# Three edits to a two-layer streaming encoder step: the order of the first tile's work, three copies out of PSUM in place of three sums, and a V load moved behind a K load

## The chip, the cores and the metric

The program runs on one core of one Trainium2 chip. The metric is the device time of one execution in microseconds: 1293.45 us is the median of three runs of the kernel before (1292.77 to 1294.03).

## What is computed

One inference step of a trunk with two layers, for two groups of rows that share all weights: a prompt of 512 rows and a sample group of 8 x 16 = 128 rows, together 640 rows of 1024 numbers, held as five tiles of 128 rows. Layer 0 mixes rows by chunked gating, layer 1 by attention with a forget bias over 16 heads, where the sample rows also read 256 cached rows of K and V for each of 8 sequences. Cut to what matters here:

```python
for i in range(DEPTH):                       # DEPTH = 2
    hp = rms_norm(xp, norm_pre[i])           # the same for the sample rows
    if i % N_MIXERS == 0:
        op, _ = gmlp_branch(hp, ...)
    else:
        qp, kp, vp, zp, lfp = fox_project(hp, fox_w_in[j], fox_b_f[j])
        op = (fox_attend_prompt(qp, kp, vp, lfp) * jax.nn.silu(zp)) @ fox_w_out[j]
        # sample rows: fox_attend_sample with cache_fox_k, cache_fox_v, cache_fox_logf
    xp = xp + rms_norm(op, norm_post[i])
    xp = xp + jax.nn.sigmoid(xp @ ple_w_gate[i]) * (p_prompt[i] @ ple_w_proj[i])
```

## The kernel before

**Split products.** Every fp32 factor of a large product is held as a high part (a ScalarE copy into a reduced fp32 format) and a low part (VectorE: source minus high part). `split` (line 286) makes both, and `mm3` (line 270) sums three matmuls of the parts in PSUM; lines 272 to 274 are most of TensorE's work. So each weight costs ScalarE one pass (line 289, or 292 with a scale) and VectorE one (line 290 or 293) before TensorE can use it.

**Seven products.** The large projections of both layers use a scheme that makes a 2 x 2 block product from seven block products in place of eight (`seven_products`, line 558). On the weights' side its sums are made by GpSimd (line 211). On the side of the activations the normalised rows h, transposed and stored split as `h_hi` and `h_lo`, are cut into four quarters: `quarter(i, j)` holds channels of half i (`c` in the transposes, 512 of 1024) and rows of half j (320 of 640). `right_operands` (line 428) first restores the four quarters as hi + lo (line 434, four VectorE adds of 128 x 1280), then forms four differences (line 436) and splits three of them into the tile `tb` (`tbf` in layer 1); the fourth is split later over `quarter(0, 1)`. `sums_of_h` (line 1175) calls it at the start of layer 1.

**The start.** The first rows come in as ten half tiles on the DMA queues. For tile t VectorE and ScalarE square one half each (lines 402 and 401), GpSimd takes a power of the sum (line 302), VectorE scales the two halves (line 409), TensorE transposes four blocks for each half (line 316, PSUM banks 5 to 7 in turn), and the transposed half is split into `A`, which holds `h_hi` and `h_lo`. Between these stand the splits of the first weights (`prefetch`). Three matmuls on zeros stand ahead of all (line 388).

**Between the layers.** `tail` (line 635) ends layer 0. In its last loop each tile of the new x is normalised and transposed by `norm_to_hT` (line 320), which fills `h_hi` and `h_lo` for layer 1.

**Layer 1.** After the first v, k and q, seven passes of one loop (lines 1189 to 1193) each project z of head pair p and v, k, q of pair p + 1 (4 x 12.35 in the code's own time units), with the attention of pair p as pieces between the matmuls at given due times (`interleave`, line 357). The cached K comes as four loads for two heads and two groups of four sequences, in pieces of 128 bytes, into one buffer (`kraw`); `turn_k` (line 1052) transposes it on VectorE (line 1056) into `kt`, and only then may the next K load write. The cached V comes by `load_v` (line 1046), two DMAs of 512 KB for one group, into one buffer `vv` that the matmuls of line 1107 read. The projections' weights come on GpSimd's DMA queue (source fox_w_in), everything named here on SyncE's. The forget bias of a head goes through memory (`c_sc`, `cs_sc`) and comes back to the `sff` tile or to the constants' tile `CST`; line 996 uses it, then lines 1006 and 1009 (score minus bias, minimum), 1012 (exponential), 1016 and 1017 (normalise) and 1023 (transposes on TensorE).

**What sets the order.** The program is written in one order and a scheduler with a timeline model chooses the order on each engine; `queued(e)` (line 127) ties the instructions inside it behind the one that was noted last for engine e. An engine runs its own instructions in that order and waits at each for what it needs. SyncE's DMA issues are one such row: an issue that waits holds back all later ones.

Of the kernel before, what the change touches and what calls it, by code (L numbers as in the profile page):

```python
# [57 lines left out]
def hybrid_trunk(tc, x_prompt, x_sample, ck, cv, clf, p_prompt, p_sample, norm_pre, norm_post,  # L58
# [6 lines left out]
    N_WARM = 3  # L65
# [220 lines left out]
    def split(hi, lo, src, times=None):  # L286

        if times is None:
            nc.scalar.activation(out=hi, in_=src, func=AF.Copy)  # L289
            nc.vector.tensor_tensor(out=lo, in0=src, in1=f(hi), op=ALU.subtract)  # L290
        else:
            nc.scalar.activation(out=hi, in_=src, func=AF.Copy, scale=times)
            nc.vector.scalar_tensor_tensor(out=lo, in0=src, scalar=times, in1=f(hi), op0=ALU.mult, op1=ALU.subtract)  # L293

# [16 lines left out]
    def transposed_split(src, hi_of, lo_of, banks):  # L311

        for c in range(2):
            b = bank(banks)
            for j in range(4):
                nc.tensor.transpose(out=b[:, j * P:(j + 1) * P], in_=src[:, (4 * c + j) * P:(4 * c + j + 1) * P], identity=ident)  # L316
            bv = b.rearrange("p (k n) -> p k n", k=4)
            split(hi_of(c), lo_of(c), bv)

    def norm_to_hT(x, junk, xn, gpre, t, banks):  # L320
        ss = small()
        nc.scalar.activation(out=junk, in_=x, func=AF.Square, accum_out=ss)
        rs = rstd_of(ss, RMS_EPS)
        nc.vector.scalar_tensor_tensor(out=xn, in0=x, scalar=rs, in1=gpre, op0=ALU.mult, op1=ALU.mult)

        transposed_split(xn, lambda c: h_hi[:, 4 * c:4 * c + 4, t * P:(t + 1) * P],
                         lambda c: h_lo[:, 4 * c:4 * c + 4, t * P:(t + 1) * P], banks)
# [68 lines left out]
    for h in range(2):  # L396
        nc.tensor.matmul(gb[h], ones, grow[:, h * 512:(h + 1) * 512], start=True, stop=True)
    for t in range(NT):
        x, xn = r2(t * D, D), r2(5120 + (t % 2) * D, D)
        ss = [small(), small()]  # L400
        nc.scalar.activation(out=xn[:, :512], in_=x[:, :512], func=AF.Square, accum_out=ss[0])
        nc.vector.scalar_tensor_tensor(out=xn[:, 512:], in0=x[:, 512:], scalar=1.0, in1=x[:, 512:], op0=ALU.mult, op1=ALU.mult,
                                       accum_out=ss[1])
# [3 lines left out]
        for h in range(2):  # L407
            hs = slice(h * 512, (h + 1) * 512)
            nc.vector.scalar_tensor_tensor(out=xn[:, hs], in0=x[:, hs], scalar=rs, in1=gb[h], op0=ALU.mult, op1=ALU.mult)
        transposed_split(xn, lambda c: h_hi[:, 4 * c:4 * c + 4, t * P:(t + 1) * P],  # L410
                         lambda c: h_lo[:, 4 * c:4 * c + 4, t * P:(t + 1) * P], (5, 6, 7))
        prefetch(t + 1)
# [15 lines left out]
    def right_operands(at):  # L428

        b11, b12, b21, b22, t_a = (r1(o, 1280).rearrange("p (k n) -> p k n", k=4) for o in at)  # L430
        t_b = b11
        for q, (i, j) in zip((b11, b12, b21, b22), ((0, 0), (0, 1), (1, 0), (1, 1))):
            hi, lo = quarter(i, j)
            nc.vector.tensor_tensor(out=q, in0=f(hi), in1=f(lo), op=ALU.add)
        for o, a, b, dst in ((t_a, b12, b11, 0), (t_b, b22, t_a, 1), (b21, b21, t_b, 2), (b12, b22, b12, None)):
# [3 lines left out]
        return b12  # L439
# [713 lines left out]
    def attention_pieces(p, step, s1):  # L1153
# [8 lines left out]
        if p < 7:  # L1162
            pieces += [(s1 + 18, lambda: store_y(2 * p)), (s0 + kb + 0.2, lambda: load_k(p + 1, 0, 0)), (s1 + 13.5, lambda: load_v(p + 1, 0))]
# [4 lines left out]
    def next_keys(p, t, t_new):  # L1168

        return [(t, lambda: turn_k(p, 0, 0)), (t + 0.1, lambda: load_k(p, 0, 1)), (t + 12, lambda: turn_k(p, 0, 1)),  # L1170
                (t + 12.1, lambda: load_k(p, 1, 0)), (t_new, lambda: new_k(p, 0))]
# [3 lines left out]
    def sums_of_h():  # L1175
        sums.append(right_operands((o_P, o_v + 1280, o_q, o_qp, o_z)))
# [61 lines left out]
```

## Time and profile before

| what | value |
|---|---|
| median of three runs | 1293.45 us (1292.77 to 1294.03) |
| the profiled execution | 1294.02 us, of it the span of the trace 1292.2 us |
| TensorE (PE) busy | 1272.2 us, 98% |
| VectorE (DVE) busy | 967.8 us, 75% |
| ScalarE (ACT) busy | 588.0 us, 46% |
| GpSimd (POOL) busy | 362.8 us, 28% |
| moved by DMA | 171.53 MB, of 275265 packets 188761 are under 512 B |

Times in the trace count from the start of the span. A row of the timeline gives start, duration, engine, line, operation, what it writes and reads, and in brackets how long the engine sat idle before it and what ended that. PEld is TensorE's load of the stationary factor. A "q" behind an engine's name is its sequencer, which issues DMAs. The view of windows gives the busy time of each engine in a stretch, with the number of its instructions, then the granted TensorE clock, the busy share of the 16 DMA engines and GB/s. The view of waits lists for each pair of waiting line and releaser the sum, the number of times and the longest.

### The profile page before, as it was taken

The numbers are of one execution on the slowest core, as the hardware profiler recorded it, in microseconds if no ns is written. First come the engines' busy times: TensorE is split into PE (matmuls) and PEld (weight loads), VectorE is DVE, ScalarE is ACT, GpSimd is POOL, SyncE is SP. The second block draws the span as 40 slices with busy tenths as digits, with TensorE's granted clock in tenths as the row PEclk, the third lists the DMA queues.
The fourth block names the chain that finished last, engine by engine and source line by source line (L and its number), as shares of the span: only waits on it lengthen the run. The fifth ranks groups of instructions, "written<-read, shape, count | busy, mean of one in ns | idle before, by whom it ended". The sixth has DMA issues, their size and how long they took to land. (4 is left out here: it accounts for less than half of the span.)

```text
span 1292.2 us, 21109 instructions
## 1 busy us (share of the span) xinstructions
PE 1272.2 (98%) x7873; PEld 1140.7 (88%) x7873; DVE 967.8 (75%) x1808; ACT 588.0 (46%) x1062; POOL 362.8 (28%) x328
## 2 busy tenths in 40 slices
PE   8999999999999999998999999999989999999998
PEld 6888999999988888887899999999979999788887
DVE  7844999999944375798988898989878988644643
ACT  5433555444535353454544454545444444545331
POOL 1012445453000010345444535454525430000100
PEclk9999999999999999999999999999999999999999
DMA  6432343332324212648797758787868758732111
GB/s 231 131 99 81 109 125 118 91 97 89 118 98 149 80 55 92 153 87 166 160 172 159 187 150 184 161 167 140 175 103 192 176 112 248 266 126 82 66 61 55
DMA packets 275265, 171.53 MB, mean 133 GB/s; under 512 B 188761, under 2 KB 238473, under 8 KB 275162
## 3 DMA queue, kind: packets, MB, share of 16 engines
q1 hardware_dynamic: 261170, 127.80, 36.2%
q0 software_dynamic: 10080, 36.89, 14.1%
q10 hardware_dynamic: 3912, 5.50, 1.4%
q8 instruction: 62, 1.02, 0.3%
q14 instruction: 41, 0.34, 0.1%
HBM read 148.55 MB, written 21.59 MB: 132 GB/s over the span
## 5 line engine op out<-in xcount | busy, mean ns | idle before, releaser
L272 PE MATMUL pb<-A,W 128*128 128x320 f32 (+1 forms) x752 | 240.9, 320 | 0.4 <-ACT A L289 0.4
L273 PE MATMUL pb<-A,W 128*128 128x320 f32 (+1 forms) x752 | 234.4, 312 | 1.0 <-DVE A L290 1.0
L274 PE MATMUL pb<-A,W 128*128 128x320 f32 (+1 forms) x752 | 234.0, 311 | 0.6 <-DVE W L293 0.5
L290 DVE TENSOR_TENSOR W<-RAW,W 128x1024 fp32r<-128x1024 f32 (+1 forms) x126 | 151.6, 1204 | 74.8 <-ACT W L289 72.2
L272 PE MATMUL pb<-W,A 128*128 128x512 f32 x520 | 204.4, 394 | 2.6 <-ACT A L289 2.6
L273 PE MATMUL pb<-W,A 128*128 128x512 f32 x520 | 203.1, 391 | 0.0
L274 PE MATMUL pb<-W,A 128*128 128x512 f32 x520 | 202.6, 393 | 0.0
L289 ACT ACTIVATE W<-RAW 128x1024 fp32r<-128x1024 f32 (+1 forms) x126 | 120.1, 953 | 95.7 <-PE pb L274 47.6
L273 PEld LDWEIGHTS pb<-A,W 128*128 128x128 f32 x752 | 142.1, 189 | 1.6 <-DVE A L290 1.3
L272 PEld LDWEIGHTS pb<-A,W 128*128 128x128 f32 x752 | 142.0, 189 | 1.5 <-ACT A L289 0.7
L274 PEld LDWEIGHTS pb<-A,W 128*128 128x128 f32 x752 | 141.6, 188 | 1.1 <-DVE W L293 1.1
L302 POOL TENSOR_TENSOR SML<-SML 128x1 f32<-128x1 f32 x25 | 17.7, 710 | 374.2 <-DVE SML L300 369.5
L272 PEld LDWEIGHTS pb<-W,A 128*128 128x128 f32 x520 | 98.0, 188 | 23.0 <-ACT A L289 3.4
L272 PE MATMUL pb<-tbf,W 128*128 128x320 f32 x360 | 118.1, 328 | 0.0
L274 PEld LDWEIGHTS pb<-W,A 128*128 128x128 f32 x520 | 97.9, 188 | 20.1 <-DVE SML L300 0.2
L273 PEld LDWEIGHTS pb<-W,A 128*128 128x128 f32 x520 | 97.9, 188 | 19.6
L274 PE MATMUL pb<-tbf,W 128*128 128x320 f32 x360 | 111.6, 310 | 0.0
L273 PE MATMUL pb<-tbf,W 128*128 128x320 f32 x360 | 111.4, 309 | 0.0
L211 POOL TENSOR_TENSOR sff<-RAW 128x512 f32<-128x512 f32 x46 | 60.5, 1317 | 180.4 <-DVE W L290 113.7
L564 DVE TENSOR_TENSOR R<-R,pb 128x320 f32<-128x320 f32 x184 | 86.3, 477 | 14.7 <-PE pb L274 13.4
L290 DVE TENSOR_TENSOR A<-R,A 128x640 fp32r<-128x640 f32 (+1 forms) x42 | 35.2, 873 | 58.6 <-ACT A L289 58.2
L272 PEld LDWEIGHTS pb<-tbf,W 128*128 128x128 f32 x360 | 67.7, 188 | 9.0 <-issue 5.4
(271 smaller groups left out, 2828.9 us busy)
## 6 DMA issues: line engine op xcount, KB each, us to landing
RAW<-in_fox_w_in POOLq DMA_DIRECT2D x46, 512.0 KB, 7.1
RAW<-in_gmlp_w_in SPq DMA_DIRECT2D x40, 512.0 KB
R<-in_cache_fox_k SPq DMA_DIRECT2D x128, 128.0 KB
R<-in_cache_fox_v SPq DMA_DIRECT2D x32, 512.0 KB
RAW<-in_gmlp_w_out SPq DMA_DIRECT2D x16, 512.0 KB
RAW<-in_ple_w_gate SPq DMA_DIRECT2D x16, 512.0 KB
RAW<-in_fox_w_out SPq DMA_DIRECT2D x16, 512.0 KB
R<-in_fox_w_in POOLq DMA_DIRECT2D x14, 512.0 KB, 8.2
```

The lines of the kernel that those rows point to most:

```text
L211: nc.gpsimd.tensor_tensor(out=o, in0=a, in1=b, op=op)
L272: nc.tensor.matmul(out, lh, rh, start=start, stop=False)
L273: nc.tensor.matmul(out, lh, rl, start=False, stop=False)
L274: nc.tensor.matmul(out, ll, rh, start=False, stop=stop)
L289: nc.scalar.activation(out=hi, in_=src, func=AF.Copy)
L290: nc.vector.tensor_tensor(out=lo, in0=src, in1=f(hi), op=ALU.subtract)
L302: behind["pool"] = nc.gpsimd.tensor_tensor(out=q, in0=t, in1=mhalf, op=ALU.pow)
L564: behind["dve"] = nc.vector.tensor_tensor(out=into(i, j), in0=a, in1=b, op=ALU.add)
```

## The change

Three edits.

1. **The first tile.** Four matmuls on zeros, into a bank that is not in use yet, stand on TensorE behind the first four transposes of tile 0. On ScalarE and VectorE the squares of tile 1 are tied behind the high part of tile 0's first half and behind both scalings of tile 0; the second weight unit's split is tied behind those scalings too.
2. **h of layer 1.** `norm_to_hT` copies the transposed half from PSUM once more with ScalarE, as plain fp32, into three of the four quarters that `right_operands` wants (all but channels of half 1, rows of half 0). `right_operands` in layer 1 then adds hi + lo for one quarter in place of four. These quarters lie in other places of the buffer `R1`, and the fourth difference goes to another place. Layer 0 still makes all four adds.
3. **V behind the second K load.** `load_v(p + 1, 0)` leaves its own due time (39.5) and is tied on SyncE's queue behind `load_k(p + 1, 1, 0)`, which is due at 46.1.

```diff
--- before.py
+++ after.py
@@ -62,7 +62,7 @@
     NRAW, NW = 3, 5
     N_SMALL, N_KEPT = 192, 172
     N_R1 = 17760
-    N_WARM = 3
+    N_WARM, N_FILL = 3, 4
 
     sbuf = tc.alloc_tile_pool(name="sbuf", bufs=1)
     psum = tc.alloc_tile_pool(name="psum", bufs=1, space=PSUM)
@@ -286,11 +286,12 @@
     def split(hi, lo, src, times=None):
 
         if times is None:
-            nc.scalar.activation(out=hi, in_=src, func=AF.Copy)
+            first = nc.scalar.activation(out=hi, in_=src, func=AF.Copy)
             nc.vector.tensor_tensor(out=lo, in0=src, in1=f(hi), op=ALU.subtract)
         else:
-            nc.scalar.activation(out=hi, in_=src, func=AF.Copy, scale=times)
+            first = nc.scalar.activation(out=hi, in_=src, func=AF.Copy, scale=times)
             nc.vector.scalar_tensor_tensor(out=lo, in0=src, scalar=times, in1=f(hi), op0=ALU.mult, op1=ALU.subtract)
+        return first
 
     def rstd_of(ss, eps, mean=False, keep=False):
         t = small()
@@ -308,14 +309,19 @@
     xin_p, xin_s = x_prompt[0], x_sample.rearrange("b q d -> (b q) d")
     yo_p, yo_s = y_p[0], y_s.rearrange("b q d -> (b q) d")
 
-    def transposed_split(src, hi_of, lo_of, banks):
+    def transposed_split(src, hi_of, lo_of, banks, after=None):
 
         for c in range(2):
             b = bank(banks)
             for j in range(4):
-                nc.tensor.transpose(out=b[:, j * P:(j + 1) * P], in_=src[:, (4 * c + j) * P:(4 * c + j + 1) * P], identity=ident)
+                behind["pe"] = nc.tensor.transpose(out=b[:, j * P:(j + 1) * P], in_=src[:, (4 * c + j) * P:(4 * c + j + 1) * P], identity=ident)
             bv = b.rearrange("p (k n) -> p k n", k=4)
-            split(hi_of(c), lo_of(c), bv)
+            hi = split(hi_of(c), lo_of(c), bv)
+            if after is not None:
+                after(c, hi, bv)
+
+    KEPT = {(0, 0): 12416, (0, 1): 5120, (1, 1): 6400}
+    HT = TOK // 2
 
     def norm_to_hT(x, junk, xn, gpre, t, banks):
         ss = small()
@@ -323,8 +329,15 @@
         rs = rstd_of(ss, RMS_EPS)
         nc.vector.scalar_tensor_tensor(out=xn, in0=x, scalar=rs, in1=gpre, op0=ALU.mult, op1=ALU.mult)
 
+        def keep(c, hi, bv):
+            for j in range(2):
+                a, b = max(t * P, j * HT), min((t + 1) * P, (j + 1) * HT)
+                if a < b and (c, j) in KEPT:
+                    q = r1(KEPT[c, j], 1280).rearrange("p (k n) -> p k n", k=4)
+                    nc.scalar.activation(out=q[:, :, a - j * HT:b - j * HT], in_=bv[:, :, a - t * P:b - t * P], func=AF.Copy)
+
         transposed_split(xn, lambda c: h_hi[:, 4 * c:4 * c + 4, t * P:(t + 1) * P],
-                         lambda c: h_lo[:, 4 * c:4 * c + 4, t * P:(t + 1) * P], banks)
+                         lambda c: h_lo[:, 4 * c:4 * c + 4, t * P:(t + 1) * P], banks, keep)
 
     h_hi, h_lo = (A[:, z:z + 5120].rearrange("p (k n) -> p k n", k=8) for z in (0, 5120))
 
@@ -395,21 +408,31 @@
     gb = PB[3], PB[4]
     for h in range(2):
         nc.tensor.matmul(gb[h], ones, grow[:, h * 512:(h + 1) * 512], start=True, stop=True)
+
+    def first_tile(c, hi, bv):
+        if c == 0:
+            behind["act"] = hi
+            for i in range(N_FILL):
+                with queued("pe"):
+                    behind["pe"] = nc.tensor.matmul(PB[2][:, :256], warm[:, :P], warm[:, 256:], start=True, stop=True)
+
     for t in range(NT):
         x, xn = r2(t * D, D), r2(5120 + (t % 2) * D, D)
         ss = [small(), small()]
-        nc.scalar.activation(out=xn[:, :512], in_=x[:, :512], func=AF.Square, accum_out=ss[0])
-        nc.vector.scalar_tensor_tensor(out=xn[:, 512:], in0=x[:, 512:], scalar=1.0, in1=x[:, 512:], op0=ALU.mult, op1=ALU.mult,
-                                       accum_out=ss[1])
+        with queued(*["act", "dve"] * (t == 1)):
+            nc.scalar.activation(out=xn[:, :512], in_=x[:, :512], func=AF.Square, accum_out=ss[0])
+            nc.vector.scalar_tensor_tensor(out=xn[:, 512:], in0=x[:, 512:], scalar=1.0, in1=x[:, 512:], op0=ALU.mult, op1=ALU.mult,
+                                           accum_out=ss[1])
         sq = small()
         nc.vector.tensor_tensor(out=sq, in0=ss[0], in1=ss[1], op=ALU.add)
         rs = rstd_of(sq, RMS_EPS)
         for h in range(2):
             hs = slice(h * 512, (h + 1) * 512)
-            nc.vector.scalar_tensor_tensor(out=xn[:, hs], in0=x[:, hs], scalar=rs, in1=gb[h], op0=ALU.mult, op1=ALU.mult)
+            behind["dve"] = nc.vector.scalar_tensor_tensor(out=xn[:, hs], in0=x[:, hs], scalar=rs, in1=gb[h], op0=ALU.mult, op1=ALU.mult)
         transposed_split(xn, lambda c: h_hi[:, 4 * c:4 * c + 4, t * P:(t + 1) * P],
-                         lambda c: h_lo[:, 4 * c:4 * c + 4, t * P:(t + 1) * P], (5, 6, 7))
-        prefetch(t + 1)
+                         lambda c: h_lo[:, 4 * c:4 * c + 4, t * P:(t + 1) * P], (5, 6, 7), first_tile if t == 0 else None)
+        with queued(*["dve"] * (t == 0)):
+            prefetch(t + 1)
 
 
     o_X, o_ln, o_sum, o_th = 14208, 15232, 16256, 17216
@@ -425,18 +448,20 @@
     def right_sum(i):
         return tuple(TB[:, z:z + 4 * HT].rearrange("p (k n) -> p k n", k=4) for z in (i * 2560, i * 2560 + 1280))
 
-    def right_operands(at):
+    def right_operands(at, ready=()):
 
         b11, b12, b21, b22, t_a = (r1(o, 1280).rearrange("p (k n) -> p k n", k=4) for o in at)
         t_b = b11
+        last = t_a if ready else b12
         for q, (i, j) in zip((b11, b12, b21, b22), ((0, 0), (0, 1), (1, 0), (1, 1))):
-            hi, lo = quarter(i, j)
-            nc.vector.tensor_tensor(out=q, in0=f(hi), in1=f(lo), op=ALU.add)
-        for o, a, b, dst in ((t_a, b12, b11, 0), (t_b, b22, t_a, 1), (b21, b21, t_b, 2), (b12, b22, b12, None)):
+            if (i, j) not in ready:
+                hi, lo = quarter(i, j)
+                nc.vector.tensor_tensor(out=q, in0=f(hi), in1=f(lo), op=ALU.add)
+        for o, a, b, dst in ((t_a, b12, b11, 0), (t_b, b22, t_a, 1), (b21, b21, t_b, 2), (last, b22, b12, None)):
             nc.vector.tensor_tensor(out=o, in0=a, in1=b, op=ALU.subtract)
             if dst is not None:
                 split(*right_sum(dst), o)
-        return b12
+        return last
 
 
     def v_at(p, t):
@@ -1160,20 +1185,25 @@
         for hh in range(2):
             pieces += prompt_times(2 * p + hh, t0 + 4 * step * hh, step)
         if p < 7:
-            pieces += [(s1 + 18, lambda: store_y(2 * p)), (s0 + kb + 0.2, lambda: load_k(p + 1, 0, 0)), (s1 + 13.5, lambda: load_v(p + 1, 0))]
+            pieces += [(s1 + 18, lambda: store_y(2 * p)), (s0 + kb + 0.2, lambda: load_k(p + 1, 0, 0))]
         if p == 6:
             pieces += [(48, lambda: load_w0(14)), (48, lambda: load_w0(15))]
         return pieces
 
     def next_keys(p, t, t_new):
 
+        def load_second():
+            load_k(p, 1, 0)
+            with queued("sp"):
+                load_v(p, 0)
+
         return [(t, lambda: turn_k(p, 0, 0)), (t + 0.1, lambda: load_k(p, 0, 1)), (t + 12, lambda: turn_k(p, 0, 1)),
-                (t + 12.1, lambda: load_k(p, 1, 0)), (t_new, lambda: new_k(p, 0))]
+                (t + 12.1, load_second), (t_new, lambda: new_k(p, 0))]
 
     sums = []
 
     def sums_of_h():
-        sums.append(right_operands((o_P, o_v + 1280, o_q, o_qp, o_z)))
+        sums.append(right_operands((KEPT[0, 0], KEPT[0, 1], o_qp, KEPT[1, 1], o_P), KEPT))
 
     def first_k():
         with queued("sp"):
```

How this moves instructions, at three places. The rows give line, operation, what it writes and reads, the shape, and how many alike stand in a row; lines of the changed kernel are numbered anew (409 became 431, 402 became 424, 434 became 459, 436 became 461, 900 became 925, 300 became 301).

First, VectorE in the first microseconds, from the first scaling of tile 0 on (`r2a_t` holds rows and their scaled copies, `W` the split weights, `A` the split h, `pb_73` and `pb_74` the gains in PSUM, `pb_75` and `pb_76` transposed halves). Before:

```order
L409 SCALAR_TENSOR_TENSOR r2a_t<-r2a_t,SML,pb_73 128x512
L290 TENSOR_TENSOR W<-RAW,W 128x1024
L402 SCALAR_TENSOR_TENSOR r2a_t,SML<-r2a_t 128x512
L409 SCALAR_TENSOR_TENSOR r2a_t<-r2a_t,SML,pb_74 128x512
L405 TENSOR_TENSOR SML<-SML 128x1
L290 TENSOR_TENSOR A<-pb_75,A 128x4x128
L300 TENSOR_SCALAR SML<-SML 128x1
L402 SCALAR_TENSOR_TENSOR r2a_t,SML<-r2a_t 128x512
L409 SCALAR_TENSOR_TENSOR r2a_t<-r2a_t,SML,pb_73 128x512
L409 SCALAR_TENSOR_TENSOR r2a_t<-r2a_t,SML,pb_74 128x512
```

and with the change:

```order
L431 SCALAR_TENSOR_TENSOR r2a_t<-r2a_t,SML,pb_73 128x512
L431 SCALAR_TENSOR_TENSOR r2a_t<-r2a_t,SML,pb_74 128x512
L290 TENSOR_TENSOR W<-RAW,W 128x1024
L424 SCALAR_TENSOR_TENSOR r2a_t,SML<-r2a_t 128x512
L290 TENSOR_TENSOR A<-pb_75,A 128x4x128
L427 TENSOR_TENSOR SML<-SML 128x1
L424 SCALAR_TENSOR_TENSOR r2a_t,SML<-r2a_t 128x512
L301 TENSOR_SCALAR SML<-SML 128x1
L290 TENSOR_TENSOR W<-RAW,W 128x1024
L290 TENSOR_TENSOR A<-pb_76,A 128x4x128
L427 TENSOR_TENSOR SML<-SML 128x1
L431 SCALAR_TENSOR_TENSOR r2a_t<-r2a_t,SML,pb_73 128x512
```

The second scaling of tile 0 comes ahead of the weights' low part, the low part of tile 0's first half moves one place up, and the scalings of tile 1 now stand behind the second weights' low part and behind the low part of tile 0's second half.

Second, VectorE where layer 0 ends and layer 1 begins, from the last but one tile's low part on (`R_69` is the buffer with the quarters and differences, `A` the split h, `tbf` the split differences). Before:

```order
L434 TENSOR_TENSOR R_69<-A 128x1280
L290 TENSOR_TENSOR A<-pb_77,A 128x4x128
L290 TENSOR_TENSOR A<-pb_75,A 128x4x128
L900 TENSOR_TENSOR R_69<-R_69,pb_70 128x256
L434 TENSOR_TENSOR R_69<-A 128x1280
L900 TENSOR_TENSOR R_69<-R_69,pb_73 128x256
L434 TENSOR_TENSOR R_69<-A 128x1280
L436 TENSOR_TENSOR R_69<-R_69 128x1280 x3
L290 TENSOR_TENSOR tbf<-R_69,tbf 128x1280
```

and with the change:

```order
L290 TENSOR_TENSOR A<-pb_77,A 128x4x128
L290 TENSOR_TENSOR A<-pb_75,A 128x4x128
L925 TENSOR_TENSOR R_69<-R_69,pb_70 128x256
L461 TENSOR_TENSOR R_69<-R_69 128x1280
L925 TENSOR_TENSOR R_69<-R_69,pb_73 128x256
L461 TENSOR_TENSOR R_69<-R_69 128x1280
L290 TENSOR_TENSOR tbf<-R_69,tbf 128x1280
L461 TENSOR_TENSOR R_69<-R_69 128x1280
L290 TENSOR_TENSOR tbf<-R_69,tbf 128x1280
```

No add of line 434 is left in this stretch (the one that stays is made before the last tile's halves), and the differences start right behind the last tile's low part.

Third, SyncE's row in one pass of the layer 1 loop, from the last store of new K rows (`out`) on; the first four of the K loads are the first head of group 1 for the next pair, the next four its second head, and the second two V loads group 1. Before:

```order
L124 DMA out<-R_69 32x16x32
L124 DMA out<-R_69 32x4x32
L124 DMA R_69<-in_cache_fox_v 128x4x256 x2
L124 DMA R_69<-in_cache_fox_k 32x32x32 x8
L124 DMA R_69<-in_cache_fox_v 128x4x256 x2
```

and with the change:

```order
L124 DMA out<-R_69 32x16x32
L124 DMA out<-R_69 32x4x32
L124 DMA R_69<-in_cache_fox_k 32x32x32 x4
L124 DMA R_69<-in_cache_fox_v 128x4x256 x2
L124 DMA R_69<-in_cache_fox_k 32x32x32 x4
L124 DMA R_69<-in_cache_fox_v 128x4x256 x2
```

The first four K loads pass the two V loads; all else in this row stays.

## The prediction

> **What bounds the kernel now.** I read the page first, then TensorE's waits, the windows around each wait, and the timelines of the engines it waits for.
>
> ```profile
> PE 1272.2 (98%) x7873; PEld 1140.7 (88%) x7873; DVE 967.8 (75%) x1808; ACT 588.0 (46%) x1062; POOL 362.8 (28%) x328
> ```
>
> TensorE is busy for 98% of the span, so the edits can only win back what it loses: 1292.2 less 1272.2, 20 us, and what a wait costs behind itself. The waits say where this is.
>
> ```profile
> PE pb L272 <- DVE SML L1009: 5.6, 2, 3.8
> PE pb L272 <- ACT A L289: 3.1, 3, 2.4
> PE pb L1023 <- DVE R L1017: 1.3, 3, 0.9
> PE pb L273 <- DVE A L290: 1.0, 1, 1.0
> ```
>
> The largest sits in an attention score (L1009) and is really two waits. The second row is mostly the start. The windows place the rest.
>
> ```profile
> 10.00:20.00 10.00, 9.04 (x37) 6.95 (x38) 9.80 (x21) 5.66 (x10) 1.10 (x2) 0.83 0.89 333
> ...
> 520.00:560.00 40.00, 40.00 (x238) 34.15 (x237) 34.16 (x41) 19.09 (x34) 11.99 (x12) 1.00 0.58 149
> 560.00:580.00 20.00, 17.98 (x109) 16.55 (x108) 20.00 (x29) 12.22 (x18) 9.33 (x8) 1.00 0.43 76
> 580.00:600.00 20.00, 19.38 (x133) 16.65 (x132) 19.75 (x33) 8.22 (x12) 11.29 (x11) 1.00 0.91 158
> 600.00:620.00 20.00, 17.31 (x126) 16.02 (x124) 16.43 (x48) 8.83 (x19) 10.12 (x13) 1.00 0.80 161
> ...
> 950.00:960.00 10.00, 6.42 (x36) 5.25 (x37) 10.00 (x22) 2.65 (x7) 6.46 (x5) 0.83 0.42 64
> ```
>
> Three places: the first 20 us; the start of layer 1, where VectorE is full (20.00 of 20) and TensorE misses 2.02 + 0.62 + 2.69 = 5.3 us from 560 to 620; and one spot near 950, where TensorE misses 3.58 us and the granted clock falls to 0.83 on average. Each edit aims at one of them.
>
> **The V load behind the second K load.** The spot near 950, on VectorE and then on TensorE:
>
> ```profile
> 949.54 1.43 DVE L1056 STREAM_TRANSPOSE R<-R 128x256 f32<-128x256 f32 x4 [6.92 <-DMA R<-in_cache_fox_k]
> ...
> 953.42 0.47 PE L272 MATMUL pb<-W 128*128 128x384 f32 x1 [3.82 <-DVE SML L1009]
> ```
>
> VectorE waits 6.92 us for a K load, though all else in its row is ready, and TensorE then waits for a score behind that transpose. SyncE's row, here and three passes earlier:
>
> ```profile
> 656.63 0.95 SPq L124 DMA_DIRECT2D R<-in_cache_fox_v  x2
> 657.67 17.02 SPq L124 DMA_DIRECT2D R<-in_cache_fox_k  x8
> ...
> 749.90 0.94 SPq L124 DMA_DIRECT2D R<-in_cache_fox_v  x2
> ...
> 818.07 0.94 SPq L124 DMA_DIRECT2D R<-in_cache_fox_v  x2
> ...
> 886.24 1.01 SPq L124 DMA_DIRECT2D R<-in_cache_fox_v  x2
> ...
> 915.45 15.36 SPq L124 DMA_DIRECT2D out<-R  x16
> 930.90 0.96 SPq L124 DMA_DIRECT2D R<-in_cache_fox_v  x2
> 931.96 21.21 SPq L124 DMA_DIRECT2D R<-in_cache_fox_k  x8
> ...
> 960.24 2.63 SPq L124 DMA_DIRECT2D R<-in_cache_fox_v  x2
> ...
> 1028.81 0.94 SPq L124 DMA_DIRECT2D R<-in_cache_fox_v  x2
> ```
>
> The V loads at 749.90, 818.07, 886.24, 960.24 and 1028.81 are the same point of five passes. The passes last 68.17, 68.17, 74.00 and 68.57: the stall costs 5.83 + 0.40 = 6.2 us, more than the 3.8 us of the wait, because the half clock after it and the work left over cost too.
>
> Why is K late in this pass alone? The K loads of the next pair are issued from 931.96 on, behind 1 MB of V at 930.90. The DMA view of 938 to 946 (while K is awaited) and of 661 to 664 (the end of a K load that came in time):
>
> ```profile
> q0 software_dynamic: 229, 0.86, 76.7%
> q1 hardware_dynamic: 1156, 0.15, 11.7%
> ```
>
> ```profile
> q1 hardware_dynamic: 3591, 0.46, 97.0%
> q0 software_dynamic: 80, 0.33, 28.4%
> ```
>
> q1 is SyncE's queue, q0 GpSimd's, with the weights. Alone, K's small packets get 97% of the engines (3591 in 3 us); beside the weights 11.7% (1156 in 8 us). At 657 V and K were through before the weights came; at 931 V took the free time, and K fell among the weights. With the change K goes first: it takes the few microseconds that V had, V meets the weights. K's issue, at 931.96 + a few, then ends before the weights and well before 942.6 (949.54 less 6.92), when VectorE wants it. I take the whole of the stall, **6.2 us**; the bounds are 0 (K late all the same) and 6.2. What is late next? V: it is needed by the matmuls of line 1107, which the V reload at 960.24 follows directly. That leaves V about 25 us from 934, where alone it needs about 4. Moved with V are its two issues, 0.96 us on SyncE; K gains them. SyncE's wait for `turn_k` now also stands ahead of V, but in this pass the 16 stores until 930.81 hold both back anyway.
>
> [...] The rows give 1156 / 229, 5 small packets of q1 for each of q0. [...]
>
> **Three of h's four sums from PSUM.** Removed on VectorE in the full stretch are three adds of line 434:
>
> ```profile
> L434 DVE TENSOR_TENSOR R<-A 128x1280 f32<-128x1280 f32 x3 | 7.1, 2355 | 1.2 <-PE pb L316 1.2
> ...
> 573.17 2.29 DVE L290 TENSOR_TENSOR A<-R,A 128x1280 fp32r<-128x1280 f32 x1
> ...
> 596.76 0.67 DVE L846 COPY R<-pb 16x512 f32<-16x512 f32 x1
> ...
> 605.38 0.29 DVE L996 TENSOR_TENSOR R<-sff,CST 128x128 f32<-128x128 f32 x1 [3.56 <-DMA sff<-c_sc]
> ...
> 575.51 0.41 PE L273 MATMUL pb<-A,W 128*128 128x320 f32 x1 [0.99 <-DVE A L290]
> ...
> 607.02 0.44 PE L272 MATMUL pb<-W 128*128 128x384 f32 x1 [1.79 <-DVE SML L1009]
> ```
>
> They hold 7.1 us between 545 and 555, all of them ahead of the differences, and VectorE has no gap from there to 601. So everything behind comes up to 7 us sooner. The changed row also pulls the forget chain (lines 830 to 848, some 4 us here, estimated from their pieces between 577.95 and 593.28) ahead of the split of `quarter(0, 1)`, the A row at 573.17: that split then ends near 575.5 - 7.1 + 4 = 572.4, over 2 us ahead of the matmul at 575.51, whose 0.99 us goes, as do the two small waits just ahead of it. The copy of the forget sums (596.76), whose trip through memory ends VectorE's wait of 3.56 us at 605.38, comes well over 10 us sooner; so the 1.79 us at 607.02 go too. Sum of TensorE's waits at stake: about 2.0 (560 to 580), 1.8, and 0.9 of the L1023 row, 4.7; I take **4.3 us**, since new waits of a few tenths for the weights' splits are likely where VectorE stays full. Bounds: 0 (something else is just behind) and the 5.3 us of the windows.
>
> Added on ScalarE are nine copies, six of 128 x 512 and three of half that size. The nearest row is a high part from PSUM, 0.58 us below: 6 x 0.58 + 3 x about 0.35 (estimate) = 4.5 us over the last gate stage and the first v. From 520 to 560 ScalarE is busy for 19.09 of 40, so they fit. Each holds its PSUM bank 0.6 us longer, out of three in turn; TensorE was never idle there (40.00 of 40). If that cover fails, the last tile's transposes wait 0.6 us each, at most twice. I cost it at nothing.
>
> **The first tile.**
>
> ```profile
> 8.73 1.23 DVE L290 TENSOR_TENSOR W<-RAW,W 128x1024 fp32r<-128x1024 f32 x1 [1.96 <-ACT W L289]
> ...
> 9.22 0.58 ACT L289 ACTIVATE A<-pb 128x512 fp32r<-128x512 f32 x1
> ...
> 9.84 0.50 PE L272 MATMUL pb<-W,A 128*128 128x512 f32 x1 [2.36 <-ACT A L289]
> ...
> 11.21 0.68 DVE L290 TENSOR_TENSOR A<-pb,A 128x512 fp32r<-128x512 f32 x1
> ...
> 11.59 1.06 ACT L289 ACTIVATE W<-RAW 128x1024 fp32r<-128x1024 f32 x1 [1.18 <-DMA RAW<-in_gmlp_w_in]
> ...
> 12.77 1.41 DVE L409 SCALAR_TENSOR_TENSOR r2a_t<-r2a_t,SML,pb 128x512 f32<-128x512 f32 x2
> ```
>
> The high part of tile 0 no longer stands behind a square, so the first product starts about 0.6 us sooner; its low part (11.21) moves up by about 0.7, the scaling that stood before it. Against that, tile 1's scalings (12.77) now stand behind the second weights' low part, which cannot start before 11.59 + 1.06 = 12.65 and takes 1.23, and behind tile 0's second low part, 0.68: 14.5, later by 1.8 us. Meanwhile TensorE has the products of tile 0, but they wait for the same low part. VectorE, 9.80 of 10 busy, makes as much in the same time; the order alone wins little. The four matmuls on zeros run while TensorE would have waited for ScalarE (2.36 us at 9.84) and cost nothing. I take **0.2 us** gain; bounds 1.8 us loss and 1.7 us gain (0.7, and 1.0 if the clock, 0.83 from 10 to 20, stays up).
>
> **The sum.** 1294.02 (span 1292.2, 1.8 around it) - 6.2 - 4.3 - 0.2 = 1283.3 for an execution like the profiled one, which lies 0.57 above the median; against the median 1293.45: 1282.7 us.
>
> **The rivals.**
> - *K is late all the same* (the weights come sooner too, or another pass takes over the stall): for it speaks that weights are in flight more than half of the time; against, that K now goes 4 us sooner in all seven passes. 1282.7 + 6.2 = 1288.9.
> [...]
> - *Layer 1's start has a second bound just behind* (weights' arrival: the DMA share is 0.91 from 580 to 600): 1282.7 + 4.3 = 1287.0.
> - *Both fail*: 1293.2.
> - *V takes K's place, slower*: V behind K meets the weights in each pass and shares at 11.7%, where 4 us of V become over 30. It decides if weights stay in flight for more than about 21 of V's 25 us. The 0.86 MB in 8 us would bring a pass's 8 units of 512 KB in under 40 of 68 us, in lumps, which speaks against. If so, at an estimated 2.5 us for each of seven passes in line 1107: 1293.45 - 4.5 - 6.2 + 17.5 = 1300.
>
> **How the numbers follow.** Both large gains: 0.55, own range 1279 to 1286. K late all the same 0.12, turns by the page 0.03, second bound in layer 1 0.13, both fail 0.07, V late 0.10. About 0.2% (2.6 us) is what a measurement of this kernel can tell from no change. Faster by more than that: 0.55 + 0.12 + 0.03 + 0.13 = 0.83; same 0.07; slower 0.10. The range leaves out V late at the top and about a tenth at the bottom (all upper bounds together: 1293.45 - 6.2 - 5.3 - 1.7 = 1280.2, and as much again as the half clock adds to a wait): 1278 to 1293.2.
>
> **What would show it.** Right: no wait of L1056 for in_cache_fox_k over 1 us, seven even passes near 68.2 us; TensorE busy over 19 of 20 us in both windows from 560 to 580 and 600 to 620; first 20 us within 1 us of before. Wrong: line 1107's matmuls waiting for in_cache_fox_v, or TensorE waiting in 560 to 620 for a split of weights with VectorE idle.

## The result and the profile after

The changed kernel takes 1288.71 us (median of six runs, 1287.66 to 1289.38) against 1293.93 us for the kernel before in the same rounds: a ratio of 0.996, interval 0.9947 to 0.9973, 5.2 us. The forecast was 10.8 us, 1282.7 us.

First the page and TensorE's waits of the changed kernel (us in total, times, longest).

```profile
PE 1271.9 (99%) x7881; PEld 1140.2 (89%) x7881; DVE 962.9 (75%) x1805; ACT 592.3 (46%) x1071; POOL 356.6 (28%) x328
```

```profile
PE pb L272 <- DVE R L600: 2.5, 1, 2.5
PE pb L272 <- DVE SML L1034: 2.0, 1, 2.0
PE pb L1048 <- DVE R L1042: 1.7, 1, 1.7
PE pb L401 <- DVE r2a_t L393: 1.5, 1, 1.5
```

The 5.6 us behind a score have shrunk to one wait of 2.0 (L1034 was L1009, L600 was L575). A wait for L600, a sum of block products, is new. The windows say where:

```profile
10.00:20.00 10.00, 9.24 (x42) 5.86 (x40) 9.23 (x20) 6.53 (x13) 2.10 (x2) 1.00 0.92 341
...
560.00:580.00 20.00, 20.00 (x121) 17.75 (x120) 17.79 (x32) 10.23 (x15) 10.14 (x9) 1.00 0.46 78
580.00:600.00 20.00, 17.46 (x127) 16.27 (x126) 11.96 (x25) 6.73 (x11) 11.88 (x14) 1.00 0.89 181
600.00:620.00 20.00, 15.95 (x108) 13.55 (x108) 18.71 (x45) 9.62 (x22) 9.81 (x9) 1.00 0.73 122
...
950.00:960.00 10.00, 10.00 (x71) 8.36 (x70) 8.21 (x20) 4.93 (x11) 7.26 (x6) 1.00 0.50 71
```

Near 950 nothing is lost any more. At the start of layer 1 TensorE gained 2 us from 560 to 580, and lost 1.9 and 1.4 more in the next two windows. VectorE has more free time than before there (11.96 of 20, was 19.75), and still TensorE waits for it.

The ledger below is worked out from the traces of all the kernels run: the start of a matmul, less the start of the same one (by its count among those of its line and operands) in the trace of before, in us, at five times of before; minus is sooner. "Round" is the median less the median of before in the same rounds.

```
                                   at 35   500   700  1000  1285 | round
changed kernel (1 + 2 + 3)          0.97  1.38  1.08 -5.15 -5.57 | -5.2
e1  V alone (3)                    -0.16  0.00 -0.33 -6.56 -7.16 | -6.9
e2  h alone (2)                    -0.82 -0.81  3.55  3.41  4.61 | +5.3
e3  first tile alone (1)            0.79  1.19  0.32  0.18  0.92 | +2.6
e4  changed, sums by SyncE          1.04  1.47  2.47 -3.77 -4.52 | -3.6
e5  2 + 3                           0.09  0.24 -1.06 -7.29 -7.81 | -7.6
e6  1 + 3                           0.78  1.08  1.21 -5.02 -5.20 | -5.1
e7  3, zeros                        0.61  0.98  1.28 -4.96 -5.30 | -6.0
e8  changed, sums by ScalarE        1.89  2.33  1.41 -4.83 -4.39 | -5.7
e9  2 + 3, no way through memory   -0.37 -0.28 -4.55 -10.78 -10.78 | -10.8
e10 3, no way through memory       -0.81 -0.66 -3.09 -9.32 -9.53 | -9.2
e11 1 + 3, no zeros                 1.67  1.96  2.10 -4.13 -4.84 | -5.1
e12 2 + 3, sums by ScalarE         -0.63 -0.62 -0.43 -6.66 -7.12 | -7.1
```

In the changed kernel the first 35 us cost 1.0 us and the rest of layer 0 another 0.4, the start of layer 1 (500 to 700) gained 0.3, and the stretch with the late K load (700 to 1000) gained 6.2.

SyncE's row of the changed kernel has the same point of the passes as the five V loads of the prediction:

```profile
750.99 0.93 SPq L124 DMA_DIRECT2D R<-in_cache_fox_v  x2
...
819.15 0.94 SPq L124 DMA_DIRECT2D R<-in_cache_fox_v  x2
...
887.32 1.71 SPq L124 DMA_DIRECT2D R<-in_cache_fox_v  x2
...
932.30 2.23 SPq L124 DMA_DIRECT2D R<-in_cache_fox_k  x4
934.63 1.20 SPq L124 DMA_DIRECT2D R<-in_cache_fox_v  x2
...
955.49 3.15 SPq L124 DMA_DIRECT2D R<-in_cache_fox_v  x2
...
1023.65 0.94 SPq L124 DMA_DIRECT2D R<-in_cache_fox_v  x2
```

All four passes last 68.16 or 68.17 us; the one of 74.00 is gone.

And the start of layer 1: GpSimd's row (which issues the weights' loads and the sums' way through memory), VectorE's, TensorE's, and the DMA view's times from issue to landing in 578 to 612.

```profile
579.22 1.51 POOL L122 DMA_DIRECT2D RAW<-in_fox_w_in  x2
581.75 0.54 POOL L122 DMA_DIRECT2D c_sc<-R  x1
588.92 0.56 POOL L122 DMA_DIRECT2D sff<-c_sc  x1 [4.73 <-DMA c_sc<-R]
```

```profile
579.19 0.64 DVE L871 COPY R<-pb 16x512 f32<-16x512 f32 x1
...
594.87 0.29 DVE L1021 TENSOR_TENSOR R<-sff,CST 128x128 f32<-128x128 f32 x1 [7.74 <-DMA sff<-c_sc]
595.08 1.22 DVE L290 TENSOR_TENSOR W<-R,W 128x1024 fp32r<-128x1024 f32 x1
596.21 0.69 DVE L290 TENSOR_TENSOR W<-RAW,W 128x512 fp32r<-128x512 f32 x1
596.81 0.48 DVE L600 TENSOR_TENSOR R<-R,pb 128x320 f32<-128x320 f32 x1
...
597.35 0.41 PE L272 MATMUL pb<-A,W 128*128 128x320 f32 x1 [2.54 <-DVE R L600]
```

```profile
sff<-c_sc POOLq DMA_DIRECT2D x1, 256.0 KB, 5.9
...
c_sc<-R POOLq DMA_DIRECT2D x1, 32.0 KB, 6.9
```

Before, the same two took less:

```profile
sff<-c_sc POOLq DMA_DIRECT2D x1, 256.0 KB, 4.5
...
c_sc<-R POOLq DMA_DIRECT2D x1, 32.0 KB, 2.8
```

The forget sums are copied at 579.19 in place of 596.76, 17.6 us sooner, but VectorE has them back only 10.5 us sooner (594.87 for 605.38). Their write is now issued 2.5 us behind two weights' loads on the same queue. Of the 7.1 us between, the write takes 4.1 (6.9 for 2.8) and the read 1.4 (5.9 for 4.5); the other 1.6 pass between the copy and the issue of the write, ahead of which GpSimd's row has two loads. VectorE's row stands at line 1021 for 7.74 us, and behind that stand two splits of weights and the sum for which TensorE waits.

### The profile page after: what moved, and what is told of

Same layout as the page of the kernel before. It is cut to its first block, busy times and chain, and to the rows that moved or that the text cites. A ratio compares the mean times of both kernels' runs of the same rounds, so it can differ in the third digit from the quotient of the medians.

```text
span 1287.1 us, 21134 instructions
## 1 busy us (share of the span) xinstructions
PE 1271.9 (99%) x7881; PEld 1140.2 (89%) x7881; DVE 962.9 (75%) x1805; ACT 592.3 (46%) x1071; POOL 356.6 (28%) x328
## 4 chain that ended last, share of the span: by engine, by line
PE 94%; DVE 3%; DMA 2%; issue 0%; ACT 0%; SPq 0%; POOL 0%; DVEq 0%; ACTq 0%; POOLq 0%
PE pb L272 27%; PE pb L273 27%; PE pb L274 27%; PE pb L1055 3%; PE pb L1132 1%; PE pb L1048 1%; PE pb L317 1%; PE pb L1105 1%; PE pb L621 1%; DVE W L290 1%; PE pb L920 1%; DMA R<-in_cache_fox_k 1%; PE pb L933 1%; DMA RAW<-in_gmlp_w_in 1%; PE pb L1129 1%; DMA r2a_t<-in_x_prompt 0%
```

## The experiments

Each ran in five rounds beside the kernel before. The ratios' intervals are 0.0009 to 0.0015 to either side, 1.2 to 1.9 us.

**Each edit alone, and the way through memory by SyncE.** e1 is the kernel before with the two changed pieces of line 1160 and `next_keys`; e2 takes `norm_to_hT`, `right_operands` and `sums_of_h`; e3 the first loop. e4 is the changed kernel with

```diff
-        dma(c_sc, cT, nc.gpsimd)
+        dma(c_sc, cT)
-load_w0(0, nc.gpsimd) ... load_w0(1, nc.gpsimd)
+load_w0(0) ... load_w0(1)
```

> The kernel before with the third edit alone (V behind the second K load). Theory A (the three edits add up, and this one is worth the whole stall): passes of 68.2 us from line to line, no wait of the transposes for in_cache_fox_k over 1 us, 1293.9 - 6.2 = 1287.7. Rival B (this edit is worth less alone, because part of the 5.2 us came from the others): 1289 to 1292. Rival C (it is worth nothing here, K late all the same): 1293.9.

Measured: 1286.93 us, ratio 0.9943 (0.9931 to 0.9956), 6.9 us; no wait for a K load over 0.3 us. A holds: the edit is worth all of the stall, and more than the whole change.

> The kernel before with the second edit alone (three quarters of h from PSUM). Theory A (what it wins on VectorE is lost again, since the forget sums' way through memory, c_sc, now starts right behind two weights' loads on GpSimd's queue): VectorE's wait for sff<-c_sc between 6 and 9 us against 3.6 before, TensorE's losses from 560 to 640 within 1 us of before, time 1293.9 - 0.3, within 0.8. Rival B (the edit is worth its 4.3 us alone, and the V loads' new place takes it back in the first pass): 1289.6, VectorE's wait for c_sc under 3 us.

Measured: 1299.14 us, ratio 1.0041 (1.0028 to 1.0054), slower by 5.3 us. Neither theory had this time. The wait for c_sc is there (7.98 us), as A had it, but the ledger puts 4.4 us between 500 and 700, and this is most of it:

```profile
674.57 1.43 DVE L1081 STREAM_TRANSPOSE R<-R 128x256 f32<-128x256 f32 x4 [5.54 <-DMA R<-in_cache_fox_k]
952.51 1.43 DVE L1081 STREAM_TRANSPOSE R<-R 128x256 f32<-128x256 f32 x4 [6.40 <-DMA R<-in_cache_fox_k]
...
678.45 0.44 PE L272 MATMUL pb<-W 128*128 128x384 f32 x1 [2.39 <-DVE SML L1034]
```

A second K load is late, in the first pass. The DMA view of 666 to 674 shows it among weights, as at 938 before:

```profile
q0 software_dynamic: 209, 0.73, 61.2%
q1 hardware_dynamic: 2052, 0.26, 20.7%
```

Its weights' load of the pass is issued at 661.73, 3.65 us behind the first K load at 658.08; before it was 662.60 behind 657.67, 4.93 us. So the edit shifts the weights against K, and another pass falls into the same hole.

> The kernel before with the first edit alone (first tile). Theory A (the loss of 1.0 us in the changed kernel is a half clock over the four gain products at 4.98 us, which depends on how long TensorE idled before them and not on the edit): if this profile shows those four products at 0.43 us a pass, the first 30 us come out 0.5 to 1.5 us sooner than before; if at 0.85, up to 1.0 later; the time of all rounds between 1292.8 and 1295. Rival B (the order itself loses): 1.0 us later, 1294.9, also with the products at 0.43.

Measured: 1296.42 us (eleven runs), ratio 1.0019 (1.0010 to 1.0028), slower by 2.6 us. The four passes of the gain products took 2.11 us in all, as fast as before (1.99), and the matmuls at 35 us still start 0.79 us later. A falls; B holds in sign, with a higher price over the rounds than the 0.9 us of its profile, which was taken of the fastest of the eleven (1294.94).

> The changed kernel with the write of the forget sums to c_sc and the first two heads' reads of it issued on SyncE's queue in place of GpSimd's. Theory A (the way through memory is long because it stands behind two weights' loads of 512 KB on one queue): the write lands within 3.5 us of its issue in place of 6.9, the first read lands before 591 in place of 594.84, VectorE's wait of 7.7 us falls under 4, TensorE's wait of 2.5 us behind it goes; 1288.7 - 3 = 1285.7, between 1284.5 and 1287.2. Rival B (something else bounds this stretch, the weights' arrival first): the read comes sooner, but the time stays within 0.8 of 1288.7 and TensorE waits as long in other places. Rival C (the reads hold K's loads back on SyncE's row): a wait for in_cache_fox_k of over 1 us near 600, and 1289 or more.

Measured: 1290.22 us, ratio 0.9969 (0.9957 to 0.998), slower than the changed kernel by its distance to before (3.6 us for 5.2). C came true:

```profile
592.03 0.78 DVE L1021 TENSOR_TENSOR R<-sff,CST 128x128 f32<-128x128 f32 x1 [5.81 <-DMA sff<-c_sc]
...
605.20 1.42 DVE L1081 STREAM_TRANSPOSE R<-R 128x256 f32<-128x256 f32 x4 [2.16 <-DMA R<-in_cache_fox_k]
...
609.08 0.45 PE L272 MATMUL pb<-W 128*128 128x384 f32 x1 [4.25 <-DVE SML L1034]
```

The sums come 2.8 us sooner, the K loads behind them in SyncE's row come later, and TensorE waits for that instead.

**Pairs of edits, the zeros alone, and the way through memory by ScalarE.** e7 has the matmuls on zeros, with the ties of squares, scalings and the second split taken off; e8 is the changed kernel with `nc.scalar` for `nc.gpsimd` in the three calls of e4.

> The second and third edit, without the first. Theory A (h from PSUM alone cost 5.3 us mostly by a second late K load, at 674 us, which V behind K takes away as well; what is left is the loss at the start of layer 1, some 0.5 us): no wait for in_cache_fox_k over 1 us, 1287.4, between 1286.6 and 1288.2. Rival B (the first tile is free here, and h costs the whole 1.8 us by which the changed kernel stands behind V alone): 1288.7. Rival C (the late K load at 674 us comes back): 1291 or more.

Measured: 1286.64 us, ratio 0.9942 (0.9928 to 0.9956); the longest wait for K 0.3 us. A holds, and with V behind K the second edit neither costs nor brings anything that can be told (0.3 us less than e1 by the medians, 0.7 by the distances to before).

> The first and third edit, without the second. Theory A (the new order of the first tile loses some 1.2 us by itself, as the profile of that edit alone showed with a full clock over the gain products): 1286.9 + 1.2 = 1288.1, between 1287.5 and 1289.3, matmuls behind 20 us shifted by 0.6 to 1.3 us against V alone. Rival B (the start's time is only the clock's chance and averages out over runs): 1286.9, within 0.4.

Measured: 1289.11 us (1288.15 to 1290.1; e1 had 1286.26 to 1287.61), ratio 0.996. A holds, at 2.2 us in the rounds and 0.9 at 35 us.

> The third edit and of the first only the four matmuls on zeros; squares, scalings and splits in the order of before. Theory A (the order of VectorE's and ScalarE's rows is what loses, the matmuls on zeros only keep the clock up): first product at most 0.2 us later than with V alone, no half clock between 11 and 15 us, 0.5 to 1.5 us sooner than V alone behind 25 us: 1285.9, between 1285.2 and 1286.5. Rival B (the matmuls on zeros are what delays the products): 1288, as with the whole first edit. Rival C (they do nothing): 1286.9, within 0.3.

Measured: 1288.23 us, ratio 0.9954 (0.9941 to 0.9966). There was no half clock from 11 to 15 us (the matmuls from 12.13 to 12.83 start 0.23 us apart, before 0.43 us from 12.54 to 13.82), and up to about 25 us the matmuls ran 1.1 us ahead of before; then twelve transposes in one row (25.08) stood ahead of products, and at 35 us it was 0.6 behind. A falls, and the time is B's, 1.3 us over e1. It isn't a clean test of the zeros: with four matmuls more the scheduler also laid out VectorE's row anew.

> The changed kernel with the write of the forget sums to c_sc and the first two heads' reads on ScalarE's queue in place of GpSimd's; K's loads on SyncE's row are not touched. Theory A (the way through memory is long because it stands behind two weights' loads on GpSimd's queue, and VectorE's row stands still behind it): first read lands before 590 in place of 594.84, VectorE's wait of 7.7 us falls under 4, TensorE's waits between 594 and 615 fall from 6.6 us in all to under 3.5: 1288.7 - 3 = 1285.7, between 1284.5 and 1287.2. Rival B (the stretch is bound by the weights' arrival or by VectorE's work): 1288.7, within 0.8, with the waits moved to splits of weights. Rival C (ScalarE, which now waits for the write to land, holds up the high parts of weights): VectorE waits for line 289's W there, 1289 or more.

Measured: 1288.46 us, ratio 0.9956 (0.9941 to 0.9971). The first two heads' sums come 3.1 us sooner and VectorE waits 4.63 us, TensorE 5.1 us from 594 to 615 in place of 6.6; the gain is too small to be told. A falls by its numbers. The DMA view of 581 to 587 and of 584 to 587 (q10 is ScalarE's queue):

```profile
q0 software_dynamic: 217, 0.82, 82.7%
q10 hardware_dynamic: 32, 0.03, 1.6%
```

```profile
q0 software_dynamic: 136, 0.49, 91.8%
```

All 32 packets of the write are through by 584, where GpSimd's queue needed until 588.6: there it did stand behind the weights. But ScalarE issues the read only at 587.07, held by something in its row that the view doesn't name (e12 has the same gap: the write is through by 580.7, the read is issued at 584.01). So the queue was one part of the delay and not the whole.

**The way through memory taken out.** e9 is e5, e10 is e1, with

```diff
-load_w0(0, nc.gpsimd)
+dma(w0_of(0), f_win[0][0, :512].partition_broadcast(P), nc.gpsimd)
```

and the same for head 1. Both leave out these two heads' own biases, so only their times are of use.

> Second and third edit, with the first two heads' reads of the forget sums taken from a row of fox_w_in in memory in place of c_sc (as many bytes to the same tiles, but nothing waits for the sums' way through memory; the biases of these two heads are wrong). Theory A (the way through memory is what now ends last at the start of layer 1, and it holds back what three sums less would bring): VectorE's wait of 6.7 us is gone, TensorE's waits from 590 to 615 fall from 3.9 us to under 1.5, 1286.6 - 3 = 1283.6, between 1282.6 and 1285. Rival B (the weights or VectorE's work bound the stretch anyway): VectorE's wait is gone, TensorE waits as long for splits or sums, 1286.6 within 0.7.

Measured: 1283.38 us, ratio 0.9921 (0.9908 to 0.9935), 3.3 us under e5. VectorE and TensorE at the place of the old waits:

```profile
584.87 0.28 DVE L1021 TENSOR_TENSOR R<-sff,CST 128x128 f32<-128x128 f32 x1
...
589.04 0.47 DVE L600 TENSOR_TENSOR R<-R,pb 128x320 f32<-128x320 f32 x1
...
602.05 0.44 PE L272 MATMUL pb<-W 128*128 128x384 f32 x1 [1.20 <-DVE SML L1034]
607.82 0.44 PE L1048 MATMUL pb<-CST,R 128*128 128x128 f32 x2 [1.71 <-DVE R L1042]
```

L1021 and L600 run without a wait. TensorE still waits 0.24 + 1.20 + 1.71 us, more than the 1.5 that A allowed; the time is A's.

> The third edit alone, with the same two reads from fox_w_in (the biases of two heads are wrong). Theory A (without the second edit VectorE's sums and the split of quarter(0, 1) bound layer 1's first 20 us, and the way through memory only the 1.8 us at 607): 1286.9 - 1.5 = 1285.4, TensorE's waits from 571 to 576 (2 us) stay, so that the second edit would be worth 2 us between this and the second and third edit with the same reads. Rival B (the second edit is worth nothing without the way through memory either): the same time as that kernel, within 0.6.

Measured: 1284.95 us, ratio 0.9932 (0.9919 to 0.9944). TensorE's waits of 0.60, 0.33 and 0.98 us from 571 to 575 stay. So the second edit is worth 1.6 us where nothing waits for the sums, 0.3 where something does; the way through memory costs 3.3 us with it and 2.0 without. A holds; e10's runs (1284.83 to 1286.04) and e9's (1282.75 to 1284.58) don't overlap.

**What of the first tile loses, and the best two edits with ScalarE's queue.** e11 is e6 with `N_FILL` 0; e12 is e5 with e8's edit.

> The first and third edit, without the four matmuls on zeros (N_FILL 0). Theory A (the order of VectorE's row is what loses, since VectorE is full there: tile 1's scalings at 14.4 us in place of 12.8): matmuls behind 35 us stand 0.6 to 1.3 us later than with V alone, 1286.9 + 1.2 = 1288.1, at most 0.5 from the kernel with the matmuls on zeros (1289.1). Rival B (the matmuls on zeros lose, in TensorE's row): 1286.9 or less. Rival C (with a half clock in the start and no matmuls on zeros it is worse than both): 1289.5 or more.

Measured: 1289.03 us, ratio 0.9959 (0.9947 to 0.9972), the time of e6. So the ties are enough for the loss, and the matmuls on zeros on top of them change nothing that can be told. At 35 us this profile is 1.67 behind, over the 1.3 of A; it has a half clock from 12.9 to 19.8 us (matmuls start 0.43 us apart from 14.46 to 15.74), and the rounds show nothing of it. VectorE's scalings of tiles 1 and 2 in e11, which stood at 12.77 and 17.76 before:

```profile
14.62 2.72 DVE L431 SCALAR_TENSOR_TENSOR r2a_t<-r2a_t,SML,pb 128x512 f32<-128x512 f32 x4 [0.54 <-POOL SML L303]
```

> Second and third edit, with the write of the forget sums and the first two heads' reads on ScalarE's queue. Theory A (as far as the reads come sooner, TensorE waits less; ScalarE's row holds the first read until 587): first read lands by 591 in place of 592.7, 1286.6 - 0.5 = 1286.1, between 1285.4 and 1286.6. Rival B (nothing is gained): 1286.6 within 0.3, or more if ScalarE's splits come late.

Measured: 1287.0 us, ratio 0.9945 (0.9933 to 0.9957). B: nothing is gained over e5. Yet the sums came 4.1 us sooner than in e5 (588.64 for 592.71), as A had asked. VectorE's row shows where that went:

```profile
588.64 1.04 DVE L1021 TENSOR_TENSOR R<-sff,CST 128x128 f32<-128x128 f32 x1 [4.51 <-DMA sff<-c_sc]
589.61 2.92 DVE L290 TENSOR_TENSOR W<-R,W 128x512 fp32r<-128x512 f32 x2
592.45 1.75 DVE L290 TENSOR_TENSOR W<-RAW,W 128x512 fp32r<-128x512 f32 x1
...
594.25 0.47 DVE L600 TENSOR_TENSOR R<-R,pb 128x320 f32<-128x320 f32 x1
```

The sum of line 600, for which TensorE waits, starts 0.4 us sooner than in e5 (594.66) and no more. A split that e5 makes ahead of the wait stands behind it here, and the same work took longer: 1.04 us for line 1021 where e5 and the changed kernel have 0.29, 1.75 for the last split where they have 0.68 and 0.69. In e8 it is alike (5.8 us from line 1021 to line 600, 1.9 in the changed kernel). Why it took longer was not tested.

Both e1 and e5 beat the kernel before and the changed kernel.

## Why the prediction was wrong

The sign was right, and the size half of what was said.

**V behind K, 6.2 us: right.** The passes are even, K waits 0.74 us at most, the ledger gives 6.2 between 700 and 1000, and e1 shows it alone. V did not become late, as the last rival had it: no matmul waits for it, though in the first pass it took 10.3 us beside the weights. The chance of 0.03 for turns between the queues is a term that no run shows; what the runs showed in its place is 1156 packets of K to 229 of the weights from 938 to 946 before, 5 to one, 207 of V to 176, 1.2 to one, from 668 to 674 in the changed kernel, and 6.9 us for the order of K and V alone (e1). One thing was missing: the hole is wider than one pass. With the second edit and V in its old place (e2) a second pass falls in, and putting V behind K is then worth 12.5 us (e5 against e2), where it is worth 6.9 alone. That is why e1, e2 and e3 sum to +1.0 and the change to -5.2. That the weights' place against K is what makes a pass late is read from the traces; no run moves the weights alone. On top of the V edit the others do add up: -6.9, 0.3 more gain by the second (e5), 2.2 lost by the first (e6), -5.0 against the -5.2 measured.

**Three sums from PSUM, 4.3 us: this step failed.** Its first half held: the split of `quarter(0, 1)` ended at 574.0, TensorE's waits from 571 to 576 went (20.00 of 20), and the copies on ScalarE cost nothing (TensorE 40.00 of 40 from 520 to 560). What failed is: "The copy of the forget sums (596.76), whose trip through memory ends VectorE's wait of 3.56 us at 605.38, comes well over 10 us sooner; so the 1.79 us at 607.02 go too." It moved the start of the trip and took its length, 7.7 us from issue to use, as fixed. Moved to 581.75, the write came behind two weights' loads, and the trip took 13.1 us. And VectorE came to line 1021 14.7 us sooner (587.13 for 601.82), more than the sums did, so that the wait grew to 7.74 us and held sums and splits of other work. TensorE missed 6.6 us from 560 to 620, where it had missed 5.3. This is the rival "a second bound just behind", given a chance of 0.13; its place was right, its cause not: it named the weights' arrival. e9 shows the cause: without the trip 3.3 us come back, TensorE misses 3.2 us there, and the time is 3.6 under e1, most of the 4.3. One term fails even so: the prediction counted 0.9 us of waits behind L1017 (now L1042) as gone, and this wait stands at 1.70 us in the changed kernel and at 1.71 in e9, where VectorE is busy for 19.26 of 20 us (600 to 620).

What of the trip's length is the queue, what the busy engines and what the rows of the engines that issue it stays open. Three kernels with every head's own biases have the sums 2.8 to 4.1 us sooner (e4, e8, e12), and none gains a time that can be told: in e4 the K loads came late in return, in e8 and e12 VectorE's work behind the wait took longer. Only taking out the whole wait paid.

**The first tile, a gain of 0.2 us: wrong sign.** The loss bound of 1.8 us was about what the rounds show. The prediction had tile 1's scalings later by 1.8 us, at 14.5; they came at 14.41. It then said that VectorE "makes as much in the same time; the order alone wins little", and that is what failed: the order lost. At 35 us the six kernels with the ties are 0.8 to 1.9 us behind, the six with the old start between 0.8 ahead and 0.1 behind; over the rounds it is 1.8 (e6 against e1, by the distances to before) to 2.6 (e3). A slower pace of the matmuls is not the reason: the four passes of the gain products took 3.75 us in e6 and in the changed kernel, 2.11 in e3, and all three lose as much; in e1 the matmuls started 0.43 us apart from 12.80 to 14.09 (0.23 from 16.75 on), and it loses nothing. e11 shows that the ties are enough. Which of the tied rows costs it was not taken apart, nor why the rounds show more than the start does.

## What to carry to other kernels

When an edit pulls a chain forward, read again what its DMAs will stand behind at the new time: a duration from the old place belongs to the old neighbours (here 7.7 us became 13.1). An engine with free time (here VectorE, busy for 11.96 of 20 us) can still be what others wait for, if a long wait stands in its row ahead of their work (7.74 us at line 1021). And where a transfer is in time in most passes and late in one, price the hole by all the passes that another edit could push into it (here 12.5 us with two passes in it, 6.9 with one); here removing it was worth more than the other edits together.

## What was not expected of the hardware

Among the weights the V packets (1024 bytes) fared no better here than K's (128 bytes): 11.8% of the engines in one window, 11.7% in the other. In the first pass of the changed kernel V, issued at 662.58, met weights issued at 663.68 and 664.46. The DMA view of 668 to 674, when no packet of K moved, has

```profile
q0 software_dynamic: 176, 0.66, 79.1%
q1 hardware_dynamic: 207, 0.21, 11.8%
```

11.8% is what K had from 938 to 946 before (11.7%), but with 1.2 packets for each of the weights, where K had five. By the trace's packet records V took 10.3 us in that pass (664.78 to 675.08), and 3.4 us in the same pass before (657.66 to 661.08). In the pass of 934.63 V was through at 940.5, and the weights' packets only began at 939.85. So the rival in which V is late had the share right and the time beside the weights too long.

Between the first 20 us and the last matmuls the half clock came in stretches of 3.41 us: from 953.70 to 957.11 before, from 608.21 to 611.62 in e1, and in e2 once as long and once twice that. The two windows of e2, cut to them:

```profile
955.39:962.21 6.82, 5.82 (x21) 5.62 (x21) 6.82 (x13) 2.65 (x7) 6.42 (x5) 0.50 0.45 69
678.91:682.32 3.41, 3.41 (x15) 3.41 (x15) 3.41 (x4) 1.49 (x5) 3.30 (x2) 0.50 0.39 60
```

In e2 it followed the wait of 2.39 us at 678.45, but in the changed kernel none of the waits of 2.54, 2.00 and 1.70 us (clock 1.00 from 580 to 620). In e1 it came 1.5 us behind a wait of 1.77 us, which ended at 606.71. So the length of a wait does not tell by itself whether a half clock comes; what else decides was not shown. And the same four passes of the gain products took 1.99 us in the kernel before and 3.75 us in the changed one:

```profile
4.72 1.99 PE L397 MATMUL pb<-r2a_t 128*128 128x512 f32 x4 [0.32 <-DMA r2a_t<-in_norm_pre]
```

```profile
4.98 3.75 PE L410 MATMUL pb<-r2a_t 128*128 128x512 f32 x4 [0.56 <-DMA r2a_t<-in_norm_pre]
```

Nothing of the change stands ahead of them: e1, with the old start, has 3.75 us too, and e3, with the new one, 2.11. At 35 us little is left of this, but two profiles with the same start still differ by up to 0.9 us there (0.97 in the changed kernel, 1.89 in e8). So small differences of single starts need the rounds.
